# Kept split weights for the second token half of the output projection, sums moved from GpSimd to VectorE, and a sixth early gate/up tile

## The chip, the cores and the metric

One core of a Trainium2 chip. The engines are TensorE (PE in the profile's rows; PEld is its weight load), VectorE (DVE), ScalarE (ACT), GpSimd (POOL) and SyncE (SP), whose queue issues the DMAs of this part of the program. The metric is the device time of one execution in microseconds (us), as a median over runs; lower is better.

## The reference, cut to what matters

One decoder layer over 512 tokens of width 2048 in float32: attention and a state-space mixer side by side, an output projection, and a gated MLP of width 5632.

```python
h = h + jnp.concatenate([attn_out, ssm_out], axis=-1) @ w_out[layer]
hn = _rmsnorm(h, norm2_g[layer])
h = h + (jax.nn.silu(hn @ w_gate[layer]) * (hn @ w_up[layer])) @ w_down[layer]
return _rmsnorm(h, final_g)
```

The change lies in the second half of the first line (the `ssm_out` rows of `w_out`), in the norm behind it and in the start of the gate/up product.

## The kernel before, in words

Activations are stored transposed: 128 channels on the partitions, 512 tokens along a row. `h[f]` is one of 16 such tiles. A float32 product is made of three matmuls (`mm3`, lines 109 to 111): every weight and every activation is split into a high and a low part, and hi·hi, hi·lo and lo·hi are added in PSUM. `split` (lines 90 and 91, the subtraction shown under line 50, the helper `tt`) makes the two parts: ScalarE copies the raw value to the high part, VectorE subtracts it from the raw value for the low part. `wraw` brings 128x1024 raw weights by DMA into one of four buffers; `wsplit` splits 512 of their columns into a ring of five buffers for each part (`whi`, `wlo`); `wchunk` does both halves of a raw tile.

The output projection runs as `oa` (attention channels, 512 tokens at once) and then as `os` (state-space channels), in two passes `e` over halves of 256 tokens. In each pass 16 tiles `f` take 24 matmuls of 256 columns each, VectorE adds the result to `h[f]`, ScalarE squares it, and the squares are summed in `ss2`. At the end of a pass `rstd_of` turns the sum into a factor for each token: two small matmuls (`ss`), a few tiny VectorE and ScalarE steps (`rst`), and a matmul that spreads it over the partitions (`bc`). Each tile of weights is loaded and split once in each pass. In the second pass the normalised first token half is made along the way (`first_half`: tiles `n1` and, split, `c1`), and so are weights of the first gate/up tiles (`split_early`).

Gate/up uses a seven-product scheme over halves of the channels and of the tokens: `product` 1 and 2 need only the first token half (operand `c1`, weights A and B), the products 3 to 7 need sums that contain the second half (`c2`, `c3`, `c4`, weights C to G). A product is 24 matmuls of 256 columns, 12 for each channel half `hh`. `gu_first` runs products 1 and 2 of the first five tiles ahead (48 matmuls a tile), each into a PSUM bank that is held until `gu` of the tile does the rest. Meanwhile a loop over `k` makes the operands: two norms of the second half (`x2`, `t34`), four sums and differences on GpSimd, and three splits (`c2`, `c3`, `c4`). Then `gu(0)` to `gu(4)` follow, with `down(0)` (tiles `dn`) behind `gu(4)`, then `gu(5)` and so on. `gu` also makes the sums of weights (`raw_r`) and the pieces behind the products (`gt`, `up`, `m`) on VectorE.

The order on each engine is fixed by a scheduler when the program is built; each engine works through its own list in order, and PSUM banks and buffers are given out in turn (`bank`, tags with a number of buffers).

Of the kernel before, what the change touches and what calls it, by code (L numbers as in the profile page):

```python
# [22 lines left out]
KT = 16  # L23
# [12 lines left out]
def _emit(tc, a, y):  # L36
    nc = tc.nc
    act, dve, pool, pe = nc.scalar, nc.vector, nc.gpsimd, nc.tensor
    open_pools = {}

    def opened(name, **kw):
        cm = tc.tile_pool(name=name, **kw)
        open_pools[name] = cm
        return cm.__enter__()
# [4 lines left out]
    def tt(out, in0, in1, op, eng=None):  # L49
        (eng or dve).tensor_tensor(out=out, in0=in0, in1=in1, op=op)  # L50
# [20 lines left out]
    wpool = opened("stage", bufs=1)  # L71
# [17 lines left out]
    def split(hi, lo, raw):  # L89
        act.activation(hi, raw, AF.Copy)  # L90
        tt(lo, raw, hi.bitcast(F32), ALU.subtract)

    def wraw(src, name):
        raw = wpool.tile([128, 1024], F32, tag="raw", name="raw_" + name, bufs=RAW)
        nc.sync.dma_start(raw, src)
        return raw

    def wsplit(raw, name):
        hi, lo = (wpool.tile([128, 512], F32R, tag=t, name=f"{t}_{name}", bufs=HB) for t in ("whi", "wlo"))
        split(hi, lo, raw)  # L100
        return hi, lo

    def wchunk(src, name):

        raw = wraw(src, name)
        return [wsplit(raw[:, 512 * i:512 * i + 512], f"{name}_{i}") for i in range(2)]
# [60 lines left out]
    def laid(pool_, tag, name, bufs, o):  # L167

        t = pool_.tile([128, SLOT], F32R, tag=tag, name=name, bufs=bufs)
        return t[:, o:o + 1024].rearrange("p (a b) -> p a b", a=2)  # L170
# [28 lines left out]
    for c in range(2):  # L199
        ws = []  # L200
        if c == 0:
            raw = wpool.tile([128, 1024], F32, tag="raw", name="raw_u0_0", bufs=RAW)
# [20 lines left out]
    for k in range(KT):  # L223
        if k == 0:
            act.activation(ssacc, xr[k], AF.Square)
        else:
            sq = wpool.tile([128, 512], F32, tag="sq", name=f"sq_x{k}", bufs=4)
# [69 lines left out]
    for n in (1, 2, 4):  # L297
# [4 lines left out]
        t_ = pt[:, :, :n]  # L302
# [233 lines left out]
    ring2 = opened("ring2", bufs=1, side="right")  # L536
# [21 lines left out]
    for b in range(8):  # L558
        yt = wpool.tile([128, 512], F32, tag="sq", name=f"yt{b}", bufs=4)
        nc.sync.dma_start(yt, sy[b].rearrange("p i c -> p (i c)"))  # L560
        t_ = laid(ring2, "B", f"ysp{b}", 8, 4)
# [23 lines left out]
    for h in range(NH):  # L585
# [4 lines left out]
        for step in "t0 t1 t2 p0 t3 p1 p2 p3".split():  # L590
            j = int(step[1])
            w = 512 - 128 * j
# [42 lines left out]
    ss2 = cpool.tile([128, 512], F32, tag="ss", name="ss2")  # L635
    rstd2 = ss2
    mp = opened("mlp", bufs=1)

    def comb(tag, name, pool_=None, bufs=8):

        return laid(pool_ or ring, tag, name, bufs, 52 if tag == "C" else 48).rearrange("p a (h t) -> p a h t", h=2)
# [9 lines left out]
    def split_early(f, hh):  # L651
        raw = load_first(f, hh)
        early[f, hh] = []
        for i in range(2):
            t_ = laid(ring2, "B", f"w{'AB'[i]}{f}_{hh}", 8, 0)
            split(t_[:, 0], t_[:, 1], raw[:, 512 * i:512 * i + 512])
            early[f, hh].append((t_[:, 0], t_[:, 1]))

    def norm(dst, k, es):
        return stt(dst, h[k][:, es], g2[:, k:k + 1], rstd2[:, es], ALU.mult, ALU.mult)  # L660
# [3 lines left out]
    c1, c2, c3, c4, n1 = [], [], [], [], []  # L664

    def first_half(k):
        n_ = laid(mp, "a", f"n1_{k}", 4, 0).bitcast(F32).rearrange("p a (h t) -> p a h t", h=2) if k % 2 == 0 else n1[-1][1]
        n1.append((n_[:, k % 2], n_))
        tc.keep_in_program_order(norm(n1[k][0][:, 0], k, E[0]))
        norm(n1[k][0][:, 1], k + 8, E[0])  # L670
        t_ = comb("A0", f"c1_{k}")
        split(t_[:, :, 0, :], t_[:, :, 1, :], n1[k][0])
        c1.append(t_)

    PRE = (2, 3, 4, 5)
    AT = (4, 5, 6, 7, 8, 9, 10, 11)
    for e in range(2):
        es = E[e]
        for f in range(KT):
            ps = acc(f"os{e}_{f}")  # L680
            ws = wchunk(a["w_out"][2 * f + 1], f"os{e}_{f}")
            for k in range(8):
                hi, lo = ws[k // 4]
                sl = slice(128 * (k % 4), 128 * (k % 4) + 128)
                mm3(ps[:, 0:256], hi[:, sl], lo[:, sl], ssm[k][:, :, es], k == 0, k == 7)
            tt(h[f][:, es], h[f][:, es], ps[:, 0:256], ALU.add)
            if f == 0:
                act.activation(ss2[:, es], h[f][:, es], AF.Square)
            else:
                sq = wpool.tile([128, 512], F32, tag="sq", name=f"sq_h{e}_{f}", bufs=4)[:, 0:256]  # L690
                act.activation(sq, h[f][:, es], AF.Square)
                tt(ss2[:, es], ss2[:, es], sq, ALU.add, pool)
            if e == 1 and f in PRE:
                split_early(PRE.index(f) // 2, PRE.index(f) % 2)
            if e == 1 and f in AT:
                first_half(AT.index(f))
        rstd_of(ss2[:, es], rstd2[:, es], f"2{e}")

    PR = {1: (c1, 0), 2: (c1, 1), 3: (c2, 0), 7: (c2, 1), 5: (c3, 0), 6: (c3, 1), 4: (c4, None)}
# [18 lines left out]
    def gu_first(f):  # L718

        bk = bank(f"gu{f}_0")  # L720
        for hh in range(2):
            if (f, hh) in early:
                wa, wb = early[f, hh]
            else:
                raw = load_first(f, hh)
                wa, wb = wsplit(raw[:, W0], f"A{f}_{hh}"), wsplit(raw[:, W1], f"B{f}_{hh}")
            product([bk], 1, hh, *wa)
            product([bk], 2, hh, *wb)
        return bk

    def gu(f, bank0=None):
        banks = [bank0 or bank(f"gu{f}_0")] + [bank(f"gu{f}_{i}") for i in range(1, 4)]
# [31 lines left out]
        split(o[:, 0, :], o[:, 1, :], g_)  # L764
        return o

    NEARLY = 5
    NPH = 11
    first = [gu_first(f) for f in range(NEARLY)]
    for k in range(8):  # L770
        es = E[1]
        x_, y_, z_ = (wpool.tile([128, 2, 256], F32, tag="sq", name=f"{n}_{k}", bufs=4) for n in ("x2", "t12", "t34"))
        norm(x_[:, 0], k + 8, es)
        norm(z_[:, 0], k, es)
        tt(x_[:, 1], x_[:, 0], z_[:, 0], ALU.subtract, pool)
        t2 = comb("B", f"c2_{k}", ring2)
        split(t2[:, :, 0, :], t2[:, :, 1, :], x_)
        tt(y_[:, 0], z_[:, 0], n1[k][0][:, 0], ALU.subtract, pool)
        tt(y_[:, 1], x_[:, 0], y_[:, 0], ALU.subtract, pool)
        t3 = comb("A1", f"c3_{k}")  # L780
        split(t3[:, :, 0, :], t3[:, :, 1, :], y_)
        tt(z_[:, 1], n1[k][0][:, 1], y_[:, 1], ALU.subtract, pool)
        if k % 2 == 0:
            t4 = comb("C", f"c4_{k}", mp, 4)
            c4.append(t4)
        split(t4[:, k % 2, 0, :], t4[:, k % 2, 1, :], z_[:, 1])
        c2.append(t2)
        c3.append(t3)
# [14 lines left out]
    for p in range(NPH):  # L803
        ms = []
        for q in range(4):
            f = 4 * p + q
            ms.append(gu(f, first[f] if f < NEARLY else None))
            if q == 0 and pend is not None:
# [4 lines left out]
    ws = []  # L813
    for c in range(8):
        raw = wpool.tile([128, 1024], F32, tag="raw", name=f"raw_dl{c}", bufs=RAW)
        nc.sync.dma_start(raw, a["w_down"][8 * (NPH - 1) + c])
        hi = laid(ring2, "B", f"whi_dl{c}", 8, 0).rearrange("p a b -> p (a b)")
        lo = slot("A0", f"wlo_dl{c}").rearrange("p a b -> p (a b)")
# [3 lines left out]
    for e in range(2):  # L822
        es = slice(256 * e, 256 * e + 256)
# [97 lines left out]
```

## Time and profile before

| | |
|---|---|
| time, median of 3 runs | 2112.76 us (2112.38 to 2114.86) |
| profiled execution | 2112.28 us, its span 2110.5 us |
| TensorE clock granted, mean share of full speed | 0.986 |

The span is the traced part of the profiled execution; 1.8 us lie outside. A busy TensorE in these rows is not TensorE at its peak, since matmuls overlap; their distance from start to start tells more.

### The profile page before, as it was taken

The page shows a single profiled execution, that of the slowest core. Times are in us where ns is not written, and L with a number is a line of the kernel's source. Part 1 is how long each engine was busy: PE and PEld are TensorE (multiplying, and loading weights), DVE is VectorE, ACT ScalarE, POOL GpSimd, SP SyncE. Part 2 cuts the span into 40 slices and gives each one's busy share as a digit, 9 for nine tenths or more (in the row PEclk, how much of TensorE's full clock was granted, in tenths as well). Part 3 has the DMA queues.
Part 4 walks back from the last instruction along what each step waited for, and adds up shares of the span by engine and source line. Part 5 has one row for each costly group of instructions (what it writes and reads, how often), then busy time and mean ns, then how long its engine had stood idle before and what let it go on. Part 6 is the DMA issues. An engine that isn't in the chain of part 4 may idle for free.

```text
span 2110.5 us, 35164 instructions
## 1 busy us (share of the span) xinstructions
PE 2053.3 (97%) x13522; PEld 1858.4 (88%) x13522; DVE 1535.6 (73%) x2932; ACT 865.6 (41%) x1523; POOL 198.1 (9%) x172
## 2 busy tenths in 40 slices
PE   7899999999999979999999999999999999999996
PEld 5688888877889979899998989899998989999896
DVE  8835897555436989687786968687686868778686
ACT  5222222346325645344443535344352535444354
POOL 4533102300002360000000000000000000000002
PEclk9999999999999989999999999999999999999998
DMA  6443234623324614323232223323232332323232
GB/s 222 127 121 112 92 102 140 178 81 125 125 91 169 206 65 140 121 100 120 82 129 90 101 101 120 111 90 130 85 124 83 111 110 101 120 88 124 90 121 80
DMA packets 117193, 244.24 MB, mean 116 GB/s; under 512 B 39040, under 2 KB 57312, under 8 KB 117024
## 3 DMA queue, kind: packets, MB, share of 16 engines
q1 hardware_dynamic: 107808, 239.88, 33.8%
q10 hardware_dynamic: 9216, 2.10, 0.5%
q8 instruction: 106, 1.74, 0.3%
q14 instruction: 63, 0.52, 0.1%
HBM read 229.77 MB, written 9.03 MB: 113 GB/s over the span
## 4 chain that ended last, share of the span: by engine, by line
PE 87%; DVE 7%; issue 2%; DMA 1%; ACT 1%; SPq 0%; POOL 0%; DVEq 0%; ACTq 0%; POOLq 0%
PE gu L109 12%; PE gu L111 12%; PE gu L110 12%; PE dn L110 7%; PE dn L109 7%; PE dn L111 7%; PE lps L437 1%; PE q L111 1%; PE q L110 1%; PE oa L111 1%; PE oa L109 1%; PE oa L110 1%; PE q L109 1%; PE v L550 1%; PE v L552 1%
## 5 line engine op out<-in xcount | busy, mean ns | idle before, releaser
L110 PE MATMUL dn<-m,whi_dn 128*128 128x512 f32 x640 | 249.0, 389 | 0.0
L109 PE MATMUL dn<-m,whi_dn 128*128 128x512 f32 x640 | 248.8, 389 | 0.0
L111 PE MATMUL dn<-m,wlo_dn 128*128 128x512 f32 x640 | 248.8, 389 | 0.0
L50 DVE TENSOR_TENSOR h<-h,dn 128x512 f32<-128x512 f32 x160 | 109.9, 687 | 172.5 <-PE dn L111 171.3
L90 ACT ACTIVATE whi_dn<-raw_dn 128x512 fp32r<-128x512 f32 x160 | 100.9, 632 | 240.5 <-PE dn L110 208.2
L50 DVE TENSOR_TENSOR raw_r<-raw_r,raw_r 128x512 f32<-128x512 f32 x264 | 182.5, 691 | 2.2
L111 PEld LDWEIGHTS dn<-m,wlo_dn 128*128 128x128 f32 x640 | 120.2, 188 | 24.9
L109 PEld LDWEIGHTS dn<-m,whi_dn 128*128 128x128 f32 x640 | 120.2, 188 | 24.6
L110 PEld LDWEIGHTS dn<-m,whi_dn 128*128 128x128 f32 x640 | 120.2, 188 | 24.5
L50 POOL TENSOR_TENSOR h<-h,ssf 128x256 f32<-128x256 f32 x12 | 10.7, 920 | 1300.1 <-ACT ssf L160 1300.1
L50 DVE TENSOR_TENSOR wlo_dn<-raw_dn,whi_dn 128x512 fp32r<-128x512 f32 x160 | 109.8, 687 | 17.6 <-ACT whi_dn L90 16.5
L109 PE MATMUL gu<-c,whi_C 128*128 128x256 f32 x352 | 99.8, 284 | 1.9 <-ACT c L90 1.6
L111 PE MATMUL gu<-c,wlo_E 128*128 128x256 f32 x352 | 98.8, 281 | 2.8 <-DVE wlo_E L50 2.8
L109 PE MATMUL gu<-c,whi_D 128*128 128x256 f32 x352 | 98.3, 279 | 2.7 <-ACT whi_D L90 2.7
L109 PE MATMUL gu<-c,whi_E 128*128 128x256 f32 x352 | 98.5, 280 | 2.4 <-ACT whi_G L90 1.7
L111 PE MATMUL gu<-c,wlo_D 128*128 128x256 f32 x352 | 98.5, 280 | 2.0 <-DVE wlo_D L50 2.0
L111 PE MATMUL gu<-c,wlo_C 128*128 128x256 f32 x352 | 99.5, 283 | 0.5 <-DVE wlo_C L50 0.5
L110 PE MATMUL gu<-c,whi_C 128*128 128x256 f32 x352 | 99.6, 283 | 0.1
L110 PE MATMUL gu<-c,whi_E 128*128 128x256 f32 x352 | 98.3, 279 | 0.0
L110 PE MATMUL gu<-c,whi_D 128*128 128x256 f32 x352 | 98.0, 278 | 0.0
L109 PE MATMUL gu<-c,whi_F 128*128 128x256 f32 x352 | 97.7, 277 | 0.0
L109 PE MATMUL gu<-c,whi_G 128*128 128x256 f32 x352 | 97.5, 277 | 0.2 <-ACT whi_G L90 0.2
(323 smaller groups left out, 6673.1 us busy)
## 6 DMA issues: line engine op xcount, KB each, us to landing
raw_r<-w_gu SPq DMA_DIRECT2D x176, 512.0 KB, 3.6
raw_dn<-w_down SPq DMA_DIRECT2D x80, 512.0 KB, 4.1
raw_os<-w_out SPq DMA_DIRECT2D x32, 512.0 KB, 3.4
raw_q<-w_q SPq DMA_DIRECT2D x16, 512.0 KB, 3.5
raw_k<-w_k SPq DMA_DIRECT2D x16, 512.0 KB, 3.4
raw_v<-w_v SPq DMA_DIRECT2D x16, 512.0 KB, 3.7
raw_oa<-w_out SPq DMA_DIRECT2D x16, 512.0 KB, 3.5
raw_u<-w_u SPq DMA_DIRECT2D x15, 512.0 KB, 4.7
```

What stands on the lines that cost most here:

```text
L50: (eng or dve).tensor_tensor(out=out, in0=in0, in1=in1, op=op)
L90: act.activation(hi, raw, AF.Copy)
L109: pe.matmul(ps, wh, x[:, 0, :], start=first, stop=False)
L110: pe.matmul(ps, wh, x[:, 1, :], start=False, stop=False)
L111: pe.matmul(ps, wl, x[:, 0, :], start=False, stop=last)
L437: pe.matmul(lps[:, g, :], tm_[:, :, :, g].rearrange("p i q -> p (i q)"), U[:, 8 * b + g, :], start=True, stop=True)
L550: pe.matmul(pss[m], xs[kt][:, 0, ms], wh, start=kt == 0, stop=False)
L552: pe.matmul(pss[m], xs[kt][:, 1, ms], wh, start=False, stop=kt == 15)
```

## The change

Six of the 16 weight tiles of `os` (`KEEP`, f = 10 to 15) are split whole, 128x1024 at once, in the first pass, into buffers of their own (`kept`), and the second pass uses them again and begins with them. The running sum of squares and the four sums of an operand step go from GpSimd to VectorE. A third gate/up tile has its A and B weights split in the second pass. `gu_first` runs for six tiles; the sixth, which has no bank of its own to hold, is copied from PSUM to an SBUF tile `ev` by ScalarE.

```diff
+    KEEP = (10, 11, 12, 13, 14, 15)
+    kept = {}
+
+    def keep(f):
+        at = ("B", ring2, 8) if KEEP.index(f) < 4 else ("C", mp, 4)
+        hl = [laid(at[1], at[0], f"{t}_kept{f}", at[2], 0).rearrange("p a b -> p (a b)") for t in ("hi", "lo")]
+        raw = wraw(a["w_out"][2 * f + 1], f"os_{f}")
+        split(hl[0], hl[1], raw)
+        kept[f] = [[t[:, 512 * i:512 * i + 512] for t in hl] for i in range(2)]
+        return kept[f]
...
-            t_ = laid(ring2, "B", f"w{'AB'[i]}{f}_{hh}", 8, 0)
+            t_ = laid(*((ring2, "B") if f < 2 else (mp, "C")), f"w{'AB'[i]}{f}_{hh}", 8 if f < 2 else 4, 0)
...
-    PRE = (2, 3, 4, 5)
-    AT = (4, 5, 6, 7, 8, 9, 10, 11)
+    PRE = (1, 2, 3, 4, 11, 12)
+    AT = (3, 4, 5, 6, 7, 8, 9, 10)
     for e in range(2):
         es = E[e]
-        for f in range(KT):
+        for i, f in enumerate(KEEP + tuple(range(KEEP[0])) if e else range(KT)):
             ps = acc(f"os{e}_{f}")
-            ws = wchunk(a["w_out"][2 * f + 1], f"os{e}_{f}")
+            ws = (kept[f] if e else keep(f)) if f in KEEP else wchunk(a["w_out"][2 * f + 1], f"os{e}_{f}")
...
-                tt(ss2[:, es], ss2[:, es], sq, ALU.add, pool)
+                tt(ss2[:, es], ss2[:, es], sq, ALU.add)
...
-        return bk
+        if f < NBANK:
+            return bk
+        out = wpool.tile([128, 512], F32, tag="ev", name=f"ev{f}")
+        act.activation(out, bk, AF.Copy)
+        return out
...
-    NEARLY = 5
+    NEARLY = 6
+    NBANK = 5
...
-        tt(x_[:, 1], x_[:, 0], z_[:, 0], ALU.subtract, pool)
+        tt(x_[:, 1], x_[:, 0], z_[:, 0], ALU.subtract)
...
-        tt(y_[:, 0], z_[:, 0], n1[k][0][:, 0], ALU.subtract, pool)
-        tt(y_[:, 1], x_[:, 0], y_[:, 0], ALU.subtract, pool)
+        tt(y_[:, 0], z_[:, 0], n1[k][0][:, 0], ALU.subtract)
+        tt(y_[:, 1], x_[:, 0], y_[:, 0], ALU.subtract)
...
-        tt(z_[:, 1], n1[k][0][:, 1], y_[:, 1], ALU.subtract, pool)
+        tt(z_[:, 1], n1[k][0][:, 1], y_[:, 1], ALU.subtract)
```

What this makes of the engines' lists is seen at three places.

VectorE where the second pass of `os` begins (`os0` and `os1` are the tiles of the two passes, `wlo_os1_0_0` is the low part of the second pass's tile 0, first half). Before:

```order
L50 TENSOR_TENSOR h_5038<-h_5038,os0_14_6171 128x256
L50 TENSOR_TENSOR wlo_os1_1_0_6306<-raw_os1_1_6303,whi_os1_1_0_6305 128x512
L50 TENSOR_TENSOR wB0_0_6386<-raw_g0_0_6380,wB0_0_6386 128x512
L50 TENSOR_TENSOR wlo_os1_1_1_6310<-raw_os1_1_6303,whi_os1_1_1_6309 128x512
L50 TENSOR_TENSOR h_5038<-h_5038,os0_15_6210 128x256
L50 TENSOR_TENSOR wlo_os1_2_0_6345<-raw_os1_2_6342,whi_os1_2_0_6344 128x512
L50 TENSOR_TENSOR wlo_os1_2_1_6349<-raw_os1_2_6342,whi_os1_2_1_6348 128x512
```

The same place after the change:

```order
L50 TENSOR_TENSOR h_5038<-h_5038,os0_14_6155 128x256
L50 TENSOR_TENSOR ss2_5623<-ss2_5623,sq_h0_14_6187 128x256
L50 TENSOR_TENSOR h_5038<-h_5038,os0_15_6190 128x256
L50 TENSOR_TENSOR ss2_5623<-ss2_5623,sq_h0_15_6222 128x256
L50 TENSOR_TENSOR h_5038<-h_5038,os1_10_6241 128x256
L50 TENSOR_TENSOR wA0_0_6300<-raw_g0_0_6297,wA0_0_6300 128x512
L50 TENSOR_TENSOR wB0_0_6303<-raw_g0_0_6297,wB0_0_6303 128x512
```

Before, the splits of the second pass's first tiles stand among the last additions of the first pass; after, none does, and the additions to `ss2` stand there.

VectorE where the operands of the second token half begin (`x2`, `t34` norms; `t12` a difference; `c2` to `c4` the split operands). Before:

```order
L59 SCALAR_TENSOR_TENSOR x2_0_7294<-h_5038,g2_67,ss2_5623 128x256
L59 SCALAR_TENSOR_TENSOR t34_0_7296<-h_5038,g2_67,ss2_5623 128x256
L59 SCALAR_TENSOR_TENSOR x2_1_7312<-h_5038,g2_67,ss2_5623 128x256
L50 TENSOR_TENSOR c2_0_7300<-x2_0_7294,c2_0_7300 128x2x256
L59 SCALAR_TENSOR_TENSOR t34_1_7314<-h_5038,g2_67,ss2_5623 128x256
L50 TENSOR_TENSOR c3_0_7305<-t12_0_7295,c3_0_7305 128x2x256
L50 TENSOR_TENSOR c4_0_7309<-t34_0_7296,c4_0_7309 128x256
```

After:

```order
L59 SCALAR_TENSOR_TENSOR x2_0_7279<-h_5038,g2_67,ss2_5623 128x256
L59 SCALAR_TENSOR_TENSOR t34_0_7281<-h_5038,g2_67,ss2_5623 128x256
L50 TENSOR_TENSOR x2_0_7279<-x2_0_7279,t34_0_7281 128x256
L50 TENSOR_TENSOR t12_0_7280<-t34_0_7281,n1_0_6382 128x256
L59 SCALAR_TENSOR_TENSOR x2_1_7297<-h_5038,g2_67,ss2_5623 128x256
L50 TENSOR_TENSOR t12_0_7280<-x2_0_7279,t12_0_7280 128x256
L50 TENSOR_TENSOR c2_0_7285<-x2_0_7279,c2_0_7285 128x2x256
L50 TENSOR_TENSOR t34_0_7281<-n1_0_6382,t12_0_7280 128x256
L59 SCALAR_TENSOR_TENSOR t34_1_7299<-h_5038,g2_67,ss2_5623 128x256
L50 TENSOR_TENSOR c3_0_7290<-t12_0_7280,c3_0_7290 128x2x256
L50 TENSOR_TENSOR x2_1_7297<-x2_1_7297,t34_1_7299 128x256
L50 TENSOR_TENSOR c4_0_7294<-t34_0_7281,c4_0_7294 128x256
```

The four sums of a step now stand between its norms and splits.

TensorE where the early tiles end and the rest of tile 0 begins (`gu4_0` is the bank of tile 4). Before:

```order
L109 MATMUL gu4_0_7223<-c1_7_6808,whi_B4_1_7266 128x256
L110 MATMUL gu4_0_7223<-c1_7_6808,whi_B4_1_7266 128x256
L111 MATMUL gu4_0_7223<-c1_7_6808,wlo_B4_1_7267 128x256
L109 MATMUL gu0_3_7437<-c4_0_7309,whi_C0_0_7442 128x256
L110 MATMUL gu0_3_7437<-c4_0_7309,whi_C0_0_7442 128x256
```

After:

```order
L109 MATMUL gu5_0_7206<-c1_7_6685,whi_B5_1_7249 128x256
L110 MATMUL gu5_0_7206<-c1_7_6685,whi_B5_1_7249 128x256
L111 MATMUL gu5_0_7206<-c1_7_6685,wlo_B5_1_7250 128x256
L109 MATMUL gu0_3_7422<-c4_0_7294,whi_C0_0_7427 128x256
L110 MATMUL gu0_3_7422<-c4_0_7294,whi_C0_0_7427 128x256
```

The 48 matmuls of a sixth tile stand ahead of the first ones that need the operands. In TensorE's list the matmul `bc` of the second pass stands 31 places later than before. In VectorE's list the stretch from the first norm of the second half (`x2_0`) to the last split of an operand holds 16 norms, 38 operations of 512 columns and 8 of 256 before; 16, 41 and 40 after; in both the first split for `gu(1)` stands one or two places behind it. From `gu(6)` to the end the lists hold the same operations in the same order.

## Rows read from the trace of the kernel before

**Rows 1.** The page's first part: busy time, share of the span, instructions of each engine.

```profile
PE 2053.3 (97%) x13522; PEld 1858.4 (88%) x13522; DVE 1535.6 (73%) x2932; ACT 865.6 (41%) x1523; POOL 198.1 (9%) x172
```

**Rows 2.** Busy time by stretches: start and end, length, engines, granted clock, DMA share, GB/s.

```profile
639.00:685.00 46.00, 46.00 (x385) 45.95 (x384) 29.36 (x49) 26.54 (x49) 11.33 (x14) 1.00 0.53 181
685.00:735.00 50.00, 48.32 (x397) 47.13 (x397) 47.04 (x86) 33.05 (x65) 16.34 (x16) 1.00 0.59 201
...
745.00:795.00 50.00, 38.85 (x259) 36.23 (x258) 46.22 (x63) 22.85 (x42) 33.64 (x32) 0.83 0.18 63
...
802.00:856.00 54.00, 53.51 (x451) 52.41 (x451) 52.18 (x96) 28.33 (x49) 0.00 (x0) 1.00 0.40 139
...
1000.00:1500.00 500.00, 500.00 (x3538) 466.93 (x3537) 375.01 (x642) 208.49 (x343) 0.00 (x0) 1.00 0.31 105
```

**Rows 3.** Waits of TensorE from 740 to 802 us: total, times, longest.

```profile
PE gu L109 <- ACT whi_D L90: 2.7, 2, 1.9
PE gu L111 <- DVE wlo_E L50: 2.6, 2, 1.4
```

**Rows 4.** Timeline of TensorE at five places: start, duration, instruction.

```profile
690.44 0.28 PE L110 MATMUL os<-ssm,whi_os 128*128 128x256 f32 x1
...
698.06 0.28 PE L109 MATMUL os<-ssm,whi_os 128*128 128x256 f32 x1
...
734.60 0.28 PE L109 MATMUL gu<-c,wA 128*128 128x256 f32 x1
...
801.28 0.35 PE L109 MATMUL gu<-c,whi_E 128*128 128x256 f32 x1 [1.74 <-ACT whi_G L90]
...
856.40 0.40 PE L109 MATMUL dn<-m,whi_dn 128*128 128x512 f32 x1
```

**Rows 5.** Timeline of VectorE where the operands begin and where they end.

```profile
744.80 0.48 DVE L59 SCALAR_TENSOR_TENSOR x<-h,g,ss 128x256 f32<-128x256 f32 x1
745.20 0.48 DVE L59 SCALAR_TENSOR_TENSOR t<-h,g,ss 128x256 f32<-128x256 f32 x1
...
792.32 0.68 DVE L50 TENSOR_TENSOR raw_r<-raw_r,raw_r 128x512 f32<-128x512 f32 x1
792.92 0.68 DVE L50 TENSOR_TENSOR wlo_F<-raw_r,whi_F 128x512 fp32r<-128x512 f32 x1
793.52 1.01 DVE L50 TENSOR_TENSOR c<-t,c 128x512 fp32r<-128x512 f32 x2
794.46 0.68 DVE L50 TENSOR_TENSOR wlo_G<-raw_r,whi_G 128x512 fp32r<-128x512 f32 x1
```

**Rows 6.** Waits of VectorE from 744.7 to 794.5 us.

```profile
DVE c L50 <- ACT c L90: 3.0, 3, 1.3
DVE wlo_A L50 <- ACT whi_A L90: 0.7, 1, 0.7
DVE t L59 <- POOL t L50: 0.6, 1, 0.6
```

**Rows 7.** Groups of VectorE's instructions, 744.7 to 794.5 us: busy, mean ns.

```profile
L50 DVE TENSOR_TENSOR c<-x,c 128x512 fp32r<-128x512 f32 x8 | 7.6, 956 | 3.0 <-ACT c L90 3.0
...
L50 DVE TENSOR_TENSOR c<-t,c 128x256 fp32r<-128x256 f32 x8 | 5.4, 680 | 0.0
```

**Rows 8.** Groups of VectorE's instructions, 802 to 856 us.

```profile
L50 DVE TENSOR_TENSOR raw_r<-raw_r,raw_r 128x512 f32<-128x512 f32 x21 | 14.3, 682 | 0.1
...
L50 DVE TENSOR_TENSOR up<-up,gu 128x256 f32<-128x256 f32 x11 | 4.5, 408 | 0.0
```

**Rows 9.** Groups of GpSimd's instructions, 640 to 800 us.

```profile
L50 POOL TENSOR_TENSOR ss<-ss,sq_h 128x256 f32<-128x256 f32 x30 | 29.0, 966 | 293.4 <-ACT sq_h L691 293.3
L50 POOL TENSOR_TENSOR x<-x,t 128x256 f32<-128x256 f32 x8 | 10.8, 1346 | 17.7 <-DVE t L59 16.6 <-ACT whi_E L90 1.1
```

**Rows 10.** A group of VectorE's, 2028 to 2052 us: subtractions of 128x1024.

```profile
L50 DVE TENSOR_TENSOR wlo_dl<-raw_dl,whi_dl 128x1024 fp32r<-128x1024 f32 x8 | 9.7, 1221 | 2.6 <-ACT whi_dl L90 2.6
```

More of the change, by code (lines that the diff above doesn't have):

```diff
@@ L686, in _emit @@
             tt(h[f][:, es], h[f][:, es], ps[:, 0:256], ALU.add)
-            if f == 0:
+            if i == 0:
                 act.activation(ss2[:, es], h[f][:, es], AF.Square)
@@ L691, in _emit @@
                 act.activation(sq, h[f][:, es], AF.Square)
-                tt(ss2[:, es], ss2[:, es], sq, ALU.add, pool)
[L693 to L696, printed above, removed]
+                tt(ss2[:, es], ss2[:, es], sq, ALU.add)
+            if e == 1 and i in PRE:
+                split_early(PRE.index(i) // 2, PRE.index(i) % 2)
+            if e == 1 and i in AT:
+                first_half(AT.index(i))
         rstd_of(ss2[:, es], rstd2[:, es], f"2{e}")
```

## The prediction

> **What bounds the kernel now.** The page first: TensorE is busy for 97% of the span, VectorE for 73% and GpSimd for 9% [rows 1]. That is a mean, so I read the stretches next. From 1000 to 1500 us TensorE is busy throughout and VectorE for 375 of 500 us [rows 2]: the long middle is TensorE's, and a matmul taken out of it is time saved. Around the change it is otherwise. In a dense run of the output projection, 65 steps from 690.44 to 698.06 us, one matmul follows the other after 0.117 us [rows 4]. At that step the 50 us from 745 to 795 have room for 427 matmuls; 259 were run [rows 2], so some 168 x 0.117 = 19.7 us are lost there. In the two passes of the projection the loss is small: 385 matmuls of 393 in the first 46 us, 397 of 427 in the 50 us from 685, which is 0.9 and 3.5 us [rows 2]. From 802 to 856 us, 451 of 461 were run: 1.1 us.
>
> Who is late in the 50 us? TensorE's waits there end with splits by ScalarE and VectorE, the longest sums being 2.7 and 2.6 us [rows 3], and VectorE is busy for 46.2 of the 50 [rows 2]. VectorE's list is the limit, so I take it apart. Its first norm starts at 744.80 us; its last operand split ends where the next instruction starts, 794.46 [rows 5]: 49.7 us. An undisturbed instruction of 512 columns follows its neighbour after 0.60 us (792.32, 792.92, 793.52), a norm after 0.40 (744.80, 745.20), and two operand splits of 512 and 256 columns take 0.94 together (793.52 to 794.46), so 0.34 for 256 [rows 5]. The list between holds 38, 16 and 8 of these: 22.8 + 6.4 + 2.7 = 31.9 us. It waited for 3.0 + 0.7 + 0.6 = 4.3 us [rows 6]. The remaining 49.7 - 31.9 - 4.3 = 13.5 us went into instructions that ran long: `c<-x` of 512 columns took 956 ns in the mean and the 256-column `c<-t` 680 ns [rows 7]; after 802 us, where GpSimd does nothing, the same sizes take 682 and 408 ns [rows 8, 2]. GpSimd is busy for 33.6 us of the 50 [rows 2], with 32 additions and subtractions.
>
> **The change, part by part.** *Sums moved, operand loop.* VectorE gets 32 operations of 256 columns, which the trace does not show on it. The nearest rows are the 256-column operand split, 0.34 us a step [rows 5], and 408 ns of full duration for one that reads PSUM [rows 8]; I take 0.34, since the new ones read SBUF and stand in a queue: 32 x 0.34 = 10.9 us (13.1 by the other). What goes is GpSimd's share: the 13.5 us of lengthening, and of the waits the 3.0 us for `c`, whose ScalarE copy stood behind a GpSimd sum of 1346 ns [rows 6, 9]. Bounds: nothing of the 16.5 comes back, or 17.1 with the 0.6 of `t`; I take 16.5, because the clean and the long rows differ in GpSimd alone.
>
> [...]
>
> *Sixth early tile.* Its 48 matmuls move ahead of the point where the operands are needed; four more half splits come with it, and a net three stand in VectorE's stretch: 3 x 0.60 = 1.8 us. They leave `gu(5)`, behind `down(0)`, where TensorE never waits [rows 2]: 48 x 0.117 = 5.6 us fewer there. The copy out of PSUM is ScalarE's; the list has nine matmuls of `gu0_3` between the sixth tile and the first matmul into that bank, 9 x 0.117 = 1.1 us of cover, so I cost it at nothing (1.1 us if the cover is gone, as ScalarE's next splits queue behind it).
>
> So VectorE's stretch becomes 49.7 - 16.5 + 10.9 + 1.8 = 45.9 us.
>
> *Kept tiles, first pass.* Six whole subtractions (1221 ns [rows 10]) replace 24 half ones of 0.60 over both passes: 14.4 to 7.3 us. The 30 sums of squares add 30 x 0.34 = 10.2 us to VectorE and remove 29.0 us of GpSimd [rows 9]. The first pass has VectorE busy for 29.4 of 46 us [rows 2], so all that is hidden; nothing is gained there. *Second pass.* It lost 3.5 us; its first six tiles now need no new weights, so splits can run ahead. But VectorE was busy for 47.0 of 50 us [rows 2] and gets 15 sums and four splits of the third early tile (5.1 + 2.4) for 12 half splits (7.2): no relief in count, only in order and in contention. Between none and all of 3.5 I take 2.4. Against that `bc` stands 31 matmuls later: 3.6 us. The first norm then starts at 744.8 + 3.6 - 2.4 = 746.0 us. The six transfers that fall away from SP's queue cost nothing now.
>
> *Sum.* The last operand is ready at 746.0 + 45.9 = 791.9 instead of 794.5: 2.6 us earlier. From there to `down(0)` (TensorE's 801.28 to 856.40 [rows 4]) both engines are full (VectorE 52.2 of 54 [rows 2]) and their lists are the same, so `down(0)` starts 2.6 us earlier too. With the 5.6 us behind it: 8.2 us. The profiled execution took 2112.28 us; 2104.1 on its scale, and as the median of the runs is 0.5 higher, 2104.5.
>
> **The rivals.** *An even exchange.* The Trainium skill (Perfetto Trace Analysis, "Optimizing Scalar/DVE Operations") warns that moving operations between GpSimd and VectorE might not help, since they share a read port. As a mechanism of this kernel: VectorE gets back only as much as the sums cost it, 10.9 instead of 16.5 us, because it works in order and its splits `c` now wait for ScalarE's copy where they waited for GpSimd's chain. The stretch is 49.7 + 1.8 = 51.5 us, ends at 797.5, 3.0 late, and 2.6 of the 5.6 us are left: 2110.1. For it: 3.0 us of the waits are named as ScalarE's [rows 6]. Against it: 5.6 us of clean shortening would have to vanish.
>
> *Slower: VectorE's saturation decides.* If the long instructions are not GpSimd's doing, nothing comes back: 49.7 + 10.9 + 1.8 = 62.4 us, to 808.4, 13.9 late, less 5.6: 8.3 us slower, 2121. It decides as soon as less than 8.3 of the 16.5 us return. For it: VectorE has no slack, 46.2 of 50 us [rows 2]. Against it: the same sizes are short from 802 us on, in an equally full VectorE [rows 8].
>
> *More.* The second pass stops waiting altogether (1.1 more), the first's 0.9 goes, the last 0.6 of the waits goes, and TensorE keeps its full clock: from 745 to 795 us the granted mean is 0.83, which is 50 x 0.17 / 0.5 = 17 us at 1.2 instead of 2.4 GHz [rows 2]; most of it falls in waiting, and I give it 2 us. Together 4.6: 2100.0. Against it: TensorE will still wait in the second half of `gu(0)`, and it waited before the clock fell.
>
> **How the numbers follow.** Forecast 57% (gains of 5 to 11 us), even exchange 20% (0 to 5), more 17% (beyond 11), slower 6%. A change under 0.2%, 4.2 us, cannot be told from none. Faster: 57 + 17 and 3 of the 20 = 77%; same: 17%; slower 6%. The range reaches from 2099, the "more" case, to 2110, where the even exchange ends; about 19% lie outside.
>
> **What would show it.** Right: VectorE's 512-column instructions between the first norm and the last operand at 0.68 us each, that stretch at 45 to 47 us, no GpSimd row between 640 and 2050 us, `down(0)` starting 3 us after where it did with 48 matmuls more behind it (5.6 - 2.6), and no TensorE wait for `wlo_os` in the second pass. That start is the quick test: about 853.8 us, and `gu(6)` 8 us earlier than before. Wrong: idle time of VectorE behind ScalarE's `c` over 4 us; a wait of ScalarE on the sixth tile's bank; second-pass waits grown because sums of squares stand ahead of splits; or 512-column instructions still near 0.95 us without GpSimd.

## The result, and the profile after

The changed kernel takes 2104.03 us in the median of seven runs (2102.64 to 2108.36); the kernel before took 2114.37 us on the same chip (2112.38 to 2119.35). The ratio is 0.9949, with a 95% interval from 0.9938 to 0.9960: about 10 us faster, where 2104.5 was predicted. The profiled execution took 2103.83 us with a span of 2102.1.

The page's first part for the changed kernel, which answers to [rows 1]:

```profile
PE 2053.5 (98%) x13522; PEld 1858.7 (88%) x13522; DVE 1528.6 (73%) x2976; ACT 857.8 (41%) x1506; POOL 135.3 (6%) x110
```

TensorE does the same 13522 matmuls in the same busy time. GpSimd has 62 instructions fewer, which are the 30 sums of squares and the 32 operand sums; VectorE has 44 more and is still busy for 7 us less. That is the first sign that its instructions have become shorter: 62 sums of 418 ns add 26 us, and six whole subtractions in place of 24 half ones take away only some 9.

The stretches, answering to [rows 2] (start and end, length, engines, granted clock, DMA share, GB/s). The first `os` matmul stands at 642.14 us here and at 639.11 before, so these windows lie 3 us later; the third covers VectorE's 45 us of operands:

```profile
642.00:688.00 46.00, 46.00 (x385) 45.95 (x384) 29.70 (x52) 21.28 (x37) 0.00 (x0) 1.00 0.50 171
688.00:738.00 50.00, 50.00 (x423) 49.95 (x422) 45.38 (x99) 32.76 (x65) 0.00 (x0) 1.00 0.53 180
748.00:793.00 45.00, 38.42 (x275) 35.51 (x275) 44.72 (x97) 24.52 (x45) 0.00 (x0) 0.87 0.27 94
805.00:859.00 54.00, 53.65 (x449) 52.58 (x448) 52.22 (x98) 27.63 (x49) 0.00 (x0) 1.00 0.43 145
1003.00:1503.00 500.00, 500.00 (x3566) 467.98 (x3565) 376.33 (x643) 210.69 (x346) 0.00 (x0) 1.00 0.30 104
```

Read them from the top. The first pass is as it was. The second pass has lost its stalls: 423 matmuls in 50 us where 397 stood. In the third window VectorE now runs 97 instructions in 45 us, without a gap, where it had run 63 in 50. TensorE still loses time there, 45 us less 275 x 0.117, which is 12.8 us where it was 19.7; waits and steps at the lower clock are both in these sums (granted mean 0.87 and 0.83). The last two rows are much as before.

VectorE's timeline, answering to [rows 5], at the first norms and at the last operands:

```profile
748.21 0.48 DVE L59 SCALAR_TENSOR_TENSOR x<-h,g,ss 128x256 f32<-128x256 f32 x1 [3.62 <-ACT ss L160]
748.61 0.48 DVE L59 SCALAR_TENSOR_TENSOR t<-h,g,ss 128x256 f32<-128x256 f32 x1
749.12 0.42 DVE L50 TENSOR_TENSOR x<-x,t 128x256 f32<-128x256 f32 x1
749.47 0.42 DVE L50 TENSOR_TENSOR t<-t,n 128x256 f32<-128x256 f32 x1
749.80 0.48 DVE L59 SCALAR_TENSOR_TENSOR x<-h,g,ss 128x256 f32<-128x256 f32 x1
...
792.06 1.02 DVE L50 TENSOR_TENSOR c<-t,c 128x512 fp32r<-128x512 f32 x2
793.15 0.69 DVE L50 TENSOR_TENSOR wlo_C<-raw_r,whi_C 128x512 fp32r<-128x512 f32 x1
```

The stretch runs from 748.21 to the end of the last split, 792.06 + 1.02 = 793.08: 44.9 us, against 49.7 before (744.80 to 793.52 + 1.01). A sum takes 0.35 and 0.33 us from start to start. Its groups from 748 to 793.2 us, answering to [rows 7]:

```profile
L50 DVE TENSOR_TENSOR c<-t,c 128x512 fp32r<-128x512 f32 x8 | 5.5, 684 | 0.0
L50 DVE TENSOR_TENSOR c<-x,c 128x512 fp32r<-128x512 f32 x8 | 5.5, 684 | 0.0
...
L50 DVE TENSOR_TENSOR t<-t,n 128x256 f32<-128x256 f32 x8 | 3.4, 419 | 0.0
L50 DVE TENSOR_TENSOR t<-x,t 128x256 f32<-128x256 f32 x8 | 3.3, 418 | 0.0
L50 DVE TENSOR_TENSOR c<-t,c 128x256 fp32r<-128x256 f32 x8 | 3.3, 418 | 0.0
```

`c<-x` is down from 956 to 684 ns and the 256-column `c<-t` from 680 to 418, the durations of [rows 8]. The waits of VectorE in the same window, answering to [rows 6], are one row, and it is the one ahead of the first norm; the waits for `c`, `wlo_A` and `t` are gone:

```profile
DVE x L59 <- ACT ss L160: 3.6, 1, 3.6
```

TensorE's waits from 745 to 805 us, answering to [rows 3]. It waits for operands and for what VectorE makes (the three longest are shown), and from 688 to 738 us the same view is empty:

```profile
PE gu L110 <- DVE c L50: 4.2, 4, 1.4
PE gu L109 <- DVE gt L50: 1.6, 1, 1.6
PE gu L109 <- ACT whi_E L90: 0.9, 1, 0.9
```

Last, three places on TensorE's timeline: the first matmul of `os`, the start of `down(0)` and that of the next down block, behind `gu(5)`:

```profile
642.14 0.28 PE L109 MATMUL os<-ssm,whi_os 128*128 128x256 f32 x1
...
855.04 0.39 PE L109 MATMUL dn<-m,whi_dn 128*128 128x512 f32 x1
...
971.14 0.39 PE L109 MATMUL dn<-m,whi_dn 128*128 128x512 f32 x1
```

The same for the kernel before, first and last place (its `down(0)` is in [rows 4]):

```profile
639.11 0.28 PE L109 MATMUL os<-ssm,whi_os 128*128 128x256 f32 x1
...
978.00 0.39 PE L109 MATMUL dn<-m,whi_dn 128*128 128x512 f32 x1
```

Raw times of the two traces can't be subtracted. The work ahead of `os` is the same in both, and it ended 3.0 us later in this execution. What goes with it shows in the windows of the first 220 us, before and then after:

```profile
0.00:220.00 220.00, 198.06 (x1127) 165.15 (x1128) 140.92 (x273) 71.79 (x133) 89.53 (x74) 0.94 0.48 143
```

```profile
0.00:220.00 220.00, 199.13 (x1116) 165.72 (x1117) 138.96 (x272) 71.98 (x132) 88.11 (x73) 0.92 0.47 143
```

The mean granted clock was 0.94 and 0.92; TensorE had spent more time at the lower of its two levels (1.2 instead of 2.4 GHz), though the change touches nothing there, and had done 11 matmuls fewer. Over all profiled executions of this study the first `os` matmul lies between 639.1 and 645.2 us. From here on every landmark is therefore counted from the first `os` matmul of its own trace. So counted, `down(0)` starts at 212.9 us instead of 217.3, and the next down block at 329.0 instead of 338.9: 9.9 us earlier. The medians differ by 10.3.

### The profile page after: what moved, and what is told of

It reads as the page before. It is cut to its first block, busy times and chain, and to the rows that moved or that the text cites. A ratio compares the mean times of both kernels' runs of the same rounds, so it can differ in the third digit from the quotient of the medians.

```text
span 2102.1 us, 35023 instructions
## 1 busy us (share of the span) xinstructions
PE 2053.5 (98%) x13522; PEld 1858.7 (88%) x13522; DVE 1528.6 (73%) x2976; ACT 857.8 (41%) x1506; POOL 135.3 (6%) x110
## 4 chain that ended last, share of the span: by engine, by line
PE 92%; DVE 5%; DMA 1%; ACT 1%; issue 1%; SPq 0%; DVEq 0%; ACTq 0%
PE gu L109 13%; PE gu L110 13%; PE gu L111 13%; PE dn L110 7%; PE dn L109 7%; PE dn L111 7%; PE os L109 1%; PE q L111 1%; PE os L110 1%; PE os L111 1%; PE lps L437 1%; PE q L109 1%; PE q L110 1%; PE oa L109 1%; PE oa L110 1%; PE oa L111 1%
## 5 line engine op out<-in xcount | busy, mean ns | idle before, releaser
L50 DVE TENSOR_TENSOR wlo_dn<-raw_dn,whi_dn 128x512 fp32r<-128x512 f32 x160 | 109.9, 688 | 17.4 <-ACT whi_dn L90 16.5
L111 PE MATMUL gu<-c,wlo_G 128*128 128x256 f32 x352 | 97.3, 277 | 0.5 <-DVE wlo_G L50 0.5
L111 PE MATMUL gu<-c,wlo_F 128*128 128x256 f32 x352 | 97.7, 278 | 0.0
```

The source lines that it names most:

```text
L111: pe.matmul(ps, wl, x[:, 0, :], start=False, stop=last)
```

## The experiments

Two theories. **Reads:** GpSimd's reads lengthen VectorE's two-input instructions, and sums on GpSimd put ScalarE's copies behind them; without them VectorE regains more than the sums cost it. **Exchange:** VectorE gets back only what the sums cost it, and the gain is that of the sixth tile and the kept tiles. What was measured, in one table of landmarks read from the timelines, all but the last two columns counted from the first `os` matmul (us; "stretch" is from the start of the first norm to the end of the last operand split; "next down" is the block behind `gu(5)`):

| kernel | last `os` matmul starts | first norm | stretch | `down(0)` | next down | median | ratio to before (95%) |
|---|---|---|---|---|---|---|---|
| before | 95.4 | 105.7 | 49.7 | 217.3 | 338.9 | 2114.37 | |
| the change | 94.8 | 106.1 | 44.9 | 212.9 | 329.0 | 2104.03 | 0.9949 (0.9938 to 0.9960) |
| e1, four sums back on GpSimd | 94.8 | 106.1 | 51.3 | 219.7 | 335.8 | 2113.45 | 0.9990 (0.9980 to 1.0000) |
| e2, five early tiles | 93.9 | 105.2 | 42.4 | 209.2 | 330.8 | 2107.26 | 0.9959 (0.9945 to 0.9973) |
| e3, no kept tiles | 97.2 | 108.6 | 44.9 | 215.1 | 331.2 | 2107.24 | 0.9960 (0.9948 to 0.9972) |
| e4, squares back on GpSimd | 94.9 | 105.0 | 45.5 | 212.4 | 328.5 | 2103.15 | 0.9944 (0.9931 to 0.9958) |
| e5, before + four sums on VectorE | 96.1 | 106.6 | 43.6 | 211.8 | 333.4 | 2108.97 | 0.9974 (0.9963 to 0.9984) |
| e6, before + sixth tile | 96.1 | 106.4 | 49.3 | 221.4 | 337.5 | 2113.48 | 0.9995 (0.9984 to 1.0007) |
| e7, seven early tiles | 94.8 | 106.1 | 48.1 | 215.4 | 326.1 | 2104.53 | 0.9943 (0.9927 to 0.9960) |
| e8, control for e7 | 94.8 | 106.1 | 44.9 | 213.3 | 329.4 | 2105.20 | 0.9953 (0.9940 to 0.9967) |
| e9, idle GpSimd reads | 94.8 | 106.1 | 61.6 | 232.4 | 348.5 | 2118.89 | 1.0018 (1.0006 to 1.0030) |
| e10, idle GpSimd writes | 94.8 | 106.1 | 44.9 | 212.9 | 329.0 | 2105.14 | 0.9947 (0.9933 to 0.9961) |
| e11, e7 + squares on GpSimd | 95.4 | 105.5 | 48.4 | 215.2 | 325.9 | 2100.79 | 0.9931 (0.9917 to 0.9944) |
| e12, two of four sums on GpSimd | 94.8 | 106.1 | 48.1 | 215.7 | 331.8 | 2107.09 | 0.9964 (0.9950 to 0.9977) |

A ratio compares with the kernel before on the same chip (medians there 2115.74 us for e1 to e4, 2115.79 for e5 to e8, 2116.36 for e9 to e12). Intervals are some 5 us wide; parts of 2 us are read from the landmarks, where the changed kernel, its control and e10 agree within 0.4 us. Ahead of the first norm the scatter is larger: before, e5 and e6 have the same lists up to there and place it at 105.7, 106.6 and 106.4 us. A part that lies behind the first norm is therefore better counted from there.

**e1: the four sums of an operand step back on GpSimd, the rest of the change kept.**

```diff
-        tt(x_[:, 1], x_[:, 0], z_[:, 0], ALU.subtract)
+        tt(x_[:, 1], x_[:, 0], z_[:, 0], ALU.subtract, pool)
...
```

The other three sums are changed alike.

> The change with one part undone: the four sums of each operand step go back to GpSimd. Theory (GpSimd's reads lengthen VectorE's): the 512-column instructions between the first norm and the last operand are long again (mean over 0.8 us), that stretch grows from 44.9 us to 44.9 - 10.9 + 16.5 = about 50.5 us, and about 5.6 of the 10 us gained are lost: 0.9975 of the time before. Rival (even exchange: VectorE regains only what the sums cost it): the stretch keeps its length within 1.5 us and the time that of the change, 0.995.

The stretch went back to 51.3 us, 6.4 longer than the change's, with 32 instructions fewer on VectorE. Its groups and waits show both halves of the mechanism again. First VectorE's groups in the stretch:

```profile
L50 DVE TENSOR_TENSOR c<-x,c 128x512 fp32r<-128x512 f32 x8 | 7.1, 886 | 3.9 <-ACT c L90 3.9
L59 DVE SCALAR_TENSOR_TENSOR x<-h,g,ss 128x256 f32<-128x256 f32 x8 | 6.1, 762 | 3.6 <-ACT ss L160 3.6
L50 DVE TENSOR_TENSOR c<-t,c 128x256 fp32r<-128x256 f32 x8 | 5.5, 684 | 0.0
```

Then GpSimd's first group from 640 us on:

```profile
L50 POOL TENSOR_TENSOR x<-x,t 128x256 f32<-128x256 f32 x8 | 12.2, 1521 | 342.6 <-DVE t L59 341.5 <-ACT whi_B L90 1.1
```

`c<-x` takes 886 ns instead of 684, and VectorE waits 3.9 us for ScalarE's copies of a sum that takes GpSimd 1521 ns. By the next down block 6.75 us are lost, a little more than the 5.6 that were expected: the loop is the largest part of the change.

**e2: five early tiles, the rest of the change kept.**

```diff
-    NEARLY = 6
+    NEARLY = 5
```

> The change with five early tiles instead of six. Theory: 48 matmuls return to the tile behind the first down product (5.6 us more there) and three half splits leave VectorE's stretch (1.8 us less): 3.8 us of the gain are lost, 0.997 of the time before. Rival (the cover is worth nothing because VectorE's list decides, and the matmuls that return are hidden): no difference from the change, 0.995.

The 5.5 us behind `down(0)` came back as counted (116.1 to 121.6 us between the two down blocks). But `down(0)` itself starts 3.7 us earlier without the sixth tile, so that the landmarks show a loss of only 1.8 us. VectorE's groups of the stretch tell most of it. Without the sixth tile:

```profile
L50 DVE TENSOR_TENSOR wlo_B<-raw_g,whi_B 128x512 fp32r<-128x512 f32 x2 | 1.4, 702 | 0.0
L50 DVE TENSOR_TENSOR wlo_A<-raw_g,whi_A 128x512 fp32r<-128x512 f32 x1 | 0.7, 703 | 0.0
```

With it, in the changed kernel:

```profile
L50 DVE TENSOR_TENSOR wlo_B<-raw_g,whi_B 128x512 fp32r<-128x512 f32 x4 | 2.8, 688 | 0.0
L50 DVE TENSOR_TENSOR wlo_A<-raw_g,whi_A 128x512 fp32r<-128x512 f32 x3 | 2.1, 690 | 0.0
```

All four half splits of the sixth tile stand in the stretch that VectorE decides: 4 x 0.60 = 2.4 of the 2.5 us by which it is longer. The first norm comes 0.85 us later too, but the sixth tile did not cause that: up to `bc` TensorE's list is the same in both kernels, and in the trace of e2 its `os` matmuls follow one another faster. The first matmul of each pass in e2:

```profile
644.01 0.28 PE L109 MATMUL os<-ssm,whi_os 128*128 128x256 f32 x1
...
689.58 0.28 PE L109 MATMUL os<-ssm,hi_kept 128*128 128x256 f32 x1
```

The second pass of the change, whose first pass begins at 642.14:

```profile
688.22 0.28 PE L109 MATMUL os<-ssm,hi_kept 128*128 128x256 f32 x1
```

The 384 matmuls of the first pass take 45.57 us in e2 and 46.08 in the change, 0.1187 and 0.1200 us a step. The trace of e4 has the faster pace too, the other twelve have the slower one; why is open. Counted from the first norm, the sixth tile costs 2.85 us ahead of `down(0)` (2.5 in the stretch, 0.35 behind it), and 2.7 us are lost without it, where 3.8 were expected.

**e3: no kept tiles; the second pass loads and splits all 16 again, in the old order.**

```diff
-        for i, f in enumerate(KEEP + tuple(range(KEEP[0])) if e else range(KT)):
+        for i, f in enumerate(range(KT)):
...
-            ws = (kept[f] if e else keep(f)) if f in KEEP else wchunk(a["w_out"][2 * f + 1], f"os{e}_{f}")
+            ws = wchunk(a["w_out"][2 * f + 1], f"os{e}_{f}")
```

> The change without kept tiles: the second pass loads and splits all 16 again, in the order 0 to 15. Theory: TensorE waits again for the low parts in the second pass, as before the change 2.4 to 3.5 us, and VectorE, which now also has the sums of squares, is late by up to 3 more: 3 to 6 us lost, 0.9965 to 0.998 of the time before. Rival (the second pass is TensorE's own and the six tiles save only transfers): under 1 us lost, 0.995.

The last `os` ends 2.5 us later and the stretch behind is unchanged; 2.2 us are lost by the next down block, less than the theory's 3 to 6 and more than the rival's 1. With a scatter of up to 0.9 us ahead of the first norm in one trace each, the size is rough, and the medians (0.9960 and 0.9949) can't tell the two kernels apart. The second pass has stalls again. TensorE's waits from 688 to 743 us:

```profile
PE bc L159 <- DVE dg L54: 1.0, 1, 1.0
PE os L111 <- DVE wlo_os L50: 0.5, 1, 0.5
```

**e4: the sums of squares back on GpSimd.**

```diff
-                tt(ss2[:, es], ss2[:, es], sq, ALU.add)
+                tt(ss2[:, es], ss2[:, es], sq, ALU.add, pool)
```

> The change with the sums of squares back on GpSimd. Theory: VectorE loses 15 sums of 0.34 us in the second pass and gets about the 6 us of lengthened instructions back; the first norm's matmul stands 23 places earlier, which costs cover but starts the operands 2.7 us sooner. Net within 2 us of the change, 0.994 to 0.996. Rival (every GpSimd sum costs VectorE as much as in the operand loop, 0.5 us, on the path): 3 us or more lost, 0.9965.

Nothing is lost; the next down block even starts 0.5 us earlier. But TensorE waits again in the second pass, where the change has no wait; whether GpSimd's reads or the other order of the lists cause that is not shown. Its longest wait:

```profile
PE os L111 <- DVE wlo_os L50: 1.3, 1, 1.3
```

Against it `bc` stands 23 places earlier in TensorE's list, and this trace has the faster pace of e2. So the first norm comes 1.0 us earlier, not the 2.7 that were expected; in e11, with the same lists up to there at the usual pace, it comes 0.5 us earlier. Counted from the first norm, e4 loses 0.6 us and e11 0.3 against e7. The move of the squares is worth nothing that these runs can tell.

**e5 and e6: the kernel before with one part of the change alone**, first the four sums on VectorE (e1's diff, the other way round), then the sixth tile:

```diff
-        return bk
+        if f < NBANK:
+            return bk
+        out = wpool.tile([128, 512], F32, tag="ev", name=f"ev{f}")
+        act.activation(out, bk, AF.Copy)
+        return out
...
-    NEARLY = 5
+    NEARLY = 6
+    NBANK = 5
```

> The kernel before with one part alone: the four sums of each operand step on VectorE. Theory (GpSimd's reads lengthen VectorE's): the stretch from the first norm to the last operand falls from 49.7 to about 43.5 us with five early tiles, its 512-column instructions at 0.68 us; 5 to 6 us faster, 0.997 to 0.9975 of the time before. Rival (even exchange): the stretch stays within 1.5 us of 49.7 and the time at 1.000; the other rival (saturation): 8 us or more slower, 1.004.

> The kernel before with one part alone: a sixth early tile, copied out of its bank. Theory: 5.6 us leave the tile behind the first down product; VectorE's stretch gets four half splits, 2.4 us clean and up to 3.4 with GpSimd beside them: 2 to 3 us faster, 0.9985 to 0.999. Rival (cover worth its whole 48 matmuls, because TensorE and not VectorE sets the end): 5.6 us faster, 0.9973. Rival (hidden): 1.000.

The loop alone shortens the stretch from 49.7 to 43.6 us, though VectorE does 32 x 0.34 = 10.9 us more in it: 17.0 us of lengthening and waits went. At the next down block 5.5 us are left (6.4 counted from the first norm, which came 0.9 us later in this trace behind the same lists), 0.26% in the median. The sixth tile alone brings 1.4 us there, and its ratio can't be told from 1: the 5.5 us behind `down(0)` are there, and `down(0)` starts 4.1 us later, 0.7 of them ahead of the first norm. That the stretch would grow by 2.4 us or more was wrong: it is 0.4 us shorter (49.3). The four half splits stand in it, but five operations that stood there before (two sums into `raw_r` and one low part each of E, F and G) come behind it, and from its end to `down(0)` it takes 65.7 us instead of 61.9.

**e7 and e8: a seventh early tile.** The second `ev` buffer needs room, which is taken from two unused pads; e8 has the pads alone.

```diff
-RPAD = 992
+RPAD = 32
...
-    pad(cpool, 480)
+    pad(cpool, 416)
...
-        out = wpool.tile([128, 512], F32, tag="ev", name=f"ev{f}")
+        out = wpool.tile([128, 512], F32, tag="ev", name=f"ev{f}", bufs=2)
...
-    NEARLY = 6
+    NEARLY = 7
```

> The change with a seventh early tile, its bank copied out as the sixth's is; for the space two paddings of unused memory shrink by 960 and 64 bytes a partition. Theory: another 48 matmuls go from behind the first down product into TensorE's waits, for four half splits more in VectorE's stretch: 5.6 - 2.4 = about 3 us faster than the change, 0.9935 of the time before. Rival (VectorE sets the end and the cover is full already): no faster than the change, 0.995, or slower by the 2.4 us.

> The change with nothing but the two smaller paddings, as a control for the seventh tile. Both theories: the time of the change, 0.995; if addresses matter, another time, and then the seventh tile is judged against this one.

The pads do nothing. The seventh tile works like the sixth: 5.4 us less behind `down(0)`, 2.5 us more ahead of it, 2.9 us net in the trace (3.2 against e8). In the time it can't be told from the change.

**e9 and e10: what GpSimd does, apart from what VectorE does.** The lists of TensorE, VectorE and ScalarE are exactly those of the change. GpSimd gets 32 extra instructions into a tile that nobody uses, four at each operand step: in e9 subtractions that read a finished operand, in e10 memsets of the same 128x256, behind one subtraction of a single column that puts them at the same place. The output is that of the change; the extra work is for nothing. First e9, then e10:

```diff
+    decoy = cpool.tile([128, 256], F32, name="decoy")
...
+        for _ in range(4):
+            tt(decoy, t2[:, 0, 0, :].bitcast(F32), t2[:, 1, 0, :].bitcast(F32), ALU.subtract, pool)
```

```diff
+    decoy = cpool.tile([128, 256], F32, name="decoy")
...
+        tt(decoy[:, 0:1], t2[:, 0, 0, 0:1].bitcast(F32), t2[:, 1, 0, 0:1].bitcast(F32), ALU.subtract, pool)
+        for _ in range(4):
+            pool.memset(decoy, 0.0)
```

> The change, with 32 subtractions of 256 columns added on GpSimd, four behind each split of c2, into a scratch tile that nobody reads; VectorE's list is that of the change, and nothing waits for GpSimd. Theory (GpSimd's reads as such lengthen VectorE's two-input instructions): the stretch from the first norm to the last operand grows from 44.9 us by 11 to 14 us (32 times about 0.4), 512-column means over 0.8 us, and the start of the first down product moves by about as much; 8 us or more slower than the change. Rival (GpSimd only cost time through the chain that waited for its results): 44.9 us, and the time of the change, 0.995.

> The same, but the 32 additions on GpSimd are fills of the scratch tile with zero, which read nothing; a subtraction of one column ahead of each four keeps them in their places. The Trainium skill's rule (SBUF - State Buffer, Who interferes with whom) has only a GpSimd instruction that reads collide with a two-input VectorE instruction: the stretch stays at 44.9 us but for the eight one-column subtractions, up to 1 us. Rival (any GpSimd work collides): it grows as with the reads.

VectorE's groups of e9 in the stretch, and GpSimd's one group:

```profile
L50 DVE TENSOR_TENSOR c<-x,c 128x512 fp32r<-128x512 f32 x8 | 9.2, 1152 | 0.0
L50 DVE TENSOR_TENSOR t<-x,t 128x256 f32<-128x256 f32 x8 | 6.5, 816 | 0.0
...
L50 DVE TENSOR_TENSOR t<-t,n 128x256 f32<-128x256 f32 x8 | 3.3, 415 | 0.0
```

```profile
L50 POOL TENSOR_TENSOR decoy<-c 128x256 f32<-128x256 f32 x32 | 31.8, 995 | 359.3 <-ACT c L90 357.4
```

The same for e10:

```profile
L50 DVE TENSOR_TENSOR c<-t,c 128x512 fp32r<-128x512 f32 x8 | 5.6, 696 | 0.0
L50 DVE TENSOR_TENSOR c<-x,c 128x512 fp32r<-128x512 f32 x8 | 5.6, 694 | 0.0
```

```profile
L797 POOL MEMSET decoy<- 128x256 f32 x32 | 10.0, 312 | 1.8
L50 POOL TENSOR_TENSOR decoy<-c 128x1 f32<-128x1 f32 x8 | 6.8, 852 | 355.6 <-ACT c L90 355.6
```

Nobody waits for either. With reads the stretch grows by 16.7 us, from 44.9 to 61.6, no VectorE instruction in it waits, and `c<-x` takes 1152 ns instead of 684, `t<-x,t` 816 instead of 418, while `t<-t,n` keeps its 415. The whole gain of the change is gone and more: 1.0018. With writes the stretch is 44.9 us and the time that of the change. The two runs together decide between the theories. GpSimd was busy for a shorter time with the writes, 10.0 us of them against 31.8 of reads; but at the price of the reads, 16.7 / 31.8, these 10.0 us would have cost 5, and they cost nothing. The size is less sure than the cause: e9's profiled execution, 2124.28 us, is among the longest of its ten, which begin at 2116.28. The median of e9 lies 13.8 us above that of e10 on the same chip, while its landmarks put `down(0)` 19.5 us later, so the trace overstates the usual loss, and how much of this is in the stretch is open.

**e11: seven early tiles with the squares on GpSimd**, e7 and e4 together.

> A version to beat the change: seven early tiles and the sums of squares back on GpSimd, with the smaller paddings. If the two gains seen in the traces add up (2.9 and 0.5 us): 3 us faster than the change, 0.9935 of the time before. Rival (with the seventh tile VectorE decides and GpSimd's collisions in the second pass come on the path): the time of the change or slower, 0.995.

It has the lowest median, 2100.79 us (2099.92 to 2104.59). At the next down block it is 3.1 us ahead of the change, of which 2.9 are the seventh tile's. Its interval still overlaps that of the change, so it is not shown to be faster.

**e12: the first and the last sum of a step on GpSimd, the two between on VectorE.**

```diff
-        tt(x_[:, 1], x_[:, 0], z_[:, 0], ALU.subtract)
+        tt(x_[:, 1], x_[:, 0], z_[:, 0], ALU.subtract, pool)
...
-        tt(z_[:, 1], n1[k][0][:, 1], y_[:, 1], ALU.subtract)
+        tt(z_[:, 1], n1[k][0][:, 1], y_[:, 1], ALU.subtract, pool)
```

> The change with two of the four sums of a step (the first and the last) on GpSimd. Theory (each GpSimd sum costs VectorE about 0.42 us by collision and frees it of 0.34): 16 of them cost net little more than 1 us by themselves and the waits for the first sum's chain come on top, up to 3: the stretch at 46 to 49 us, between 44.9 and 51.3. Rival (the collision needs a queue on GpSimd, so two per step run in gaps): the stretch at 42 to 44 us, and a time below the change's.

VectorE's longest group in the stretch, and its only wait there beside the one ahead of the first norm:

```profile
L50 DVE TENSOR_TENSOR c<-t,c 128x512 fp32r<-128x512 f32 x8 | 7.7, 963 | 0.3 <-ACT c L90 0.2
```

```profile
DVE c L50 <- ACT c L90: 0.2, 1, 0.2
```

The stretch is 48.1 us. VectorE saves 16 x 0.34 = 5.4 us of sums and pays 3.2 + 5.4 = 8.6 us, nearly all of it in instructions that run long. Of the three divisions that were run with the rest of the change (none, two or four of the sums on GpSimd), the stretch is 44.9, 48.1 and 51.3 us: on the average a sum that goes to GpSimd costs more than it saves.

## Why the prediction was right

The mechanism held, and the total came 1.7 us above the 8.2 of the sum. Two terms were too small, and the share given to one part was too large. That 2104.03 lies so near the 2104.5 is luck: the gain was 2 us larger than forecast (10.3 in the medians for 8.3), and the three runs that the forecast started from lay 1.6 us below the later median of the same kernel.

- **VectorE's list sets the stretch.** Right. After the change it has no wait in it, and it is 97 instructions end to end. From its end to `down(0)` it takes 61.9 us before and 62.0 after, as the sum assumed.
- **The sums: 10.9 us added, 16.5 us back.** Right. 0.33 to 0.35 us a sum was measured. The stretch became 44.9 us where 45.9 was worked out; with 10.9 and 1.8 added, 49.7 - 44.9 + 12.7 = 17.5 us came back, 0.4 above the upper bound of 17.1: about all of the lengthening and every wait (13.5 + 4.3 = 17.8).
- **The even exchange**, given 20%, falls. e5 shows 5.5 us from the loop alone where it allows none, and e1 loses 6.75 when the loop is undone. The Trainium skill (Perfetto Trace Analysis, "Optimizing Scalar/DVE Operations") warns that offloading operations between these two engines might not help, because they share a read port. Towards GpSimd the runs agree, e1 and e12; away from it, where VectorE is the engine waited for, the move did help: a sum takes 418 ns on VectorE, against 966 to 1346 ns on GpSimd [rows 9], and GpSimd's reads are gone.
- **Slower by saturation** falls with the same rows, and e9 shows what its premise missed: with VectorE's list the same, GpSimd's reads alone made the stretch 16.7 us longer.
- **How much of GpSimd's time is lost.** The Trainium skill (SBUF — State Buffer, "Who interferes with whom") says that two-input VectorE instructions collide with GpSimd's reads and not with instructions that only write. e9 and e10 agree: 61.6 against 44.9 us. About half of GpSimd's time was lost to VectorE, not all of it: 16.7 us for 31.8 in e9, 13.5 for 33.6 before.
- **The sixth tile** was mis-sized. Behind `down(0)` 5.5 us went, as counted (5.6). But its price ahead of `down(0)` was put at three half splits, 1.8 us, and e2 measures 2.85: all four splits (2.5) and 0.35 behind. The three had been the net of the whole change's list, in which the third early tile takes one away. Net it is worth 2.7 us (2.1 in e6, both from the first norm), not 3.8. The total did not suffer, since the net of three was right for the list as a whole. The copy of its bank was costed at nothing, and no wait of TensorE up to `down(0)` names it in the change.
- **The second pass** was mis-sized the other way. All of its stalls went, not 2.4 of 3.5 us, and the first norm came 0.4 us later, not 1.2; that difference is within the scatter there (before's 105.7 is the lowest of three traces with its lists). That the kept tiles took the stalls away is e3: 2.5 us at the end of `os`. The six transfers that fell away and the third early tile were not tested apart.
- **More**, given 17%, came in part: the second pass lost its stalls and VectorE its last wait. The 0.9 us of the first pass did not go and were no wait: 385 matmuls stand in its first 46 us before and after, at 0.120 us a step instead of 0.117. And the clock still fell: the granted mean is 0.87 in VectorE's stretch after, 0.83 before.
- **The squares** were costed at nothing, and e4 agrees on the net, with a wait in the second pass against an earlier `bc`.
- **`down(0)`** came 4.4 us earlier, not 2.6: 1.0 from the stretch and 0.8 from the first norm. With 5.5 behind it that is 9.9 us instead of 8.2. Behind the first norm alone the whole change is worth 10.3 us, and the parts undone one at a time cost 6.75 (loop), 2.7 (sixth tile), 0.6 (squares) and -0.3 us (kept tiles), 9.7 together. Done alone, the loop is worth 6.4 and the sixth tile 2.1, so they hardly act on each other.
- **The quick test** was badly put: "about 853.8 us" for `down(0)` was a raw time, and 855.04 would have spoken for a smaller gain, had the 3.0 us ahead of `os` not been taken off.

Left open: why `os` has two paces (0.1187 us a step in e2 and e4, 0.1200 in the others, the change with e2's very list among them), why four of e9's ten executions took over 2122 us, and what of the few tenths behind the stretch belongs to which part.

## What to carry to other kernels

Where VectorE decides a stretch, count what GpSimd reads beside it: compare the mean duration of one VectorE group there with the same shape where GpSimd is idle, and the excess is what a move can give back, to be set against the work that moves. Where VectorE has room, the same work may stay on GpSimd. Work that is done early to shorten a later part is paid for in the stretch that it is moved ahead of, in splits on the engine that decides there. And compare two traces from the first instruction that the change can reach, not from their starts.

## What the runs showed of the hardware

- 32 GpSimd subtractions of 128x256 (995 ns each) beside a saturated VectorE made VectorE's list 16.7 us longer in the one trace of e9 (a long execution), 0.52 us each; 32 memsets of the same tile on GpSimd (312 ns each) nothing. The lengthening, waits taken off, was 13.5 us for 32 in the kernel before, 12.8 for 32 in e1 and 8.4 for 16 in e12: 0.4 to 0.5 us each.
- The loss falls on single instructions: in e9 one group of 256-column sums takes 816 ns in the mean and another 415.
- The same first 640 us of the program ended between 639.1 and 645.2 us in 14 profiled executions, more than half of the change's whole effect, with a mean granted clock of 0.94 and 0.92 over the first 220 us in the two that are shown.
- The 384 matmuls of 256 columns of the first `os` pass, at a granted clock of 1.00, followed one another after 0.1187 us in two traces and after 0.1200 in twelve.
